# Mixer A's copy of q in the order of dilation 4: from ScalarE to GpSimd

## The chip, the core and the metric

The kernel runs on one core of a Trainium2 chip. The metric is the time of one execution in microseconds (us) on that core. The core has five engines that work side by side, each through its own instructions in the program's order: TensorE (PE; PEld is its weight load), VectorE (DVE), ScalarE (ACT), GpSimd (POOL) and SyncE (SP, which only issues DMAs here). They wait for each other by semaphores.

## The reference, cut to what matters

One layer of an encoder over 2048 tokens of width 1024: RMSNorm, one input projection, two mixers side by side (A: dilated window attention; B: latent attention), an output projection, a mixture of experts, a last RMSNorm. The change lies in mixer A. It has 8 heads of 64 columns, and each head attends three times, with windows of stride 1, 4 and 16:

```python
for window, dilation in ((128, 1), (512, 4), (2048, 16)):
    qr, kr, vr = to_residue(q), to_residue(k), to_residue(v)   # order by residue modulo the dilation
    scores = einsum('bhrnqd,bhrnkd->bhrnqk', qblk, kb) * dh ** -0.5
    scores = where(valid, scores + bias, NEG_INF)
    p = exp(scores - max(scores)); l = sum(p); o = p @ vb / l
# the three outputs are merged by their log-sum-exp weights
```

## The kernel before

The stages follow each other: `phase1` (input projection), `phase3` (mixer A), `mla` (mixer B), `phase5` (output projection), `moe` with `final`. In `phase3`, q of a head comes by DMA into the tile QA16, a [128, 2048] tile of fp16 in the order of dilation 16, which holds the two fp16 halves of q on 64 partitions each. The matmuls want q in 128 adjacent columns for each window, so `perm_q` copies it twice more on chip: into QA1 (order of dilation 1) and QA4 (order of dilation 4), in four pieces of 512 columns each. For QA4 a piece is written to 512 adjacent columns and read as 16 runs of 32 columns.

The work of a head is cut into 20 units: units 0 to 3 of dilation 16 (four windows each), 4 to 11 of dilation 1 and 12 to 19 of dilation 4 (two windows each); 8 heads make 160 units. One loop runs over steps s, and each step issues six parts of a pipeline, in this order:

- for the unit s: its `perm_q` piece, if it has one (QA1 in units 0 to 3, QA4 in units 4 to 7), then `qk` (PE, lines 681 and 682, into the PSUM tile S), `soft1` (DVE, line 706: adds the bias table and takes the row's extreme, into the tiles sb and st)
- for s-1: `soft2` (POOL, lines 723 and 729: subtracts the extreme, sb into pp)
- for s-2: `soft3` (ACT, line 733: exp, in place in pp)
- for s-3: `trans` (PE, line 746: transposes pp into PT; then ACT, line 757: the upper fp16 half, phi)
- for s-4: `low` (DVE, line 763: the lower half, plo)
- for s-5: `pv` (PE, lines 783 to 785, into O; at the end of a group of units ACT, line 788, copies O out into st)

The scheduler is switched off (`tc.manual_schedule()`): each engine runs its instructions in the order in which the program issues them. S has 3 buffers, sb 3, pp 4, and QA4 has one. QA16 alternates between two places from head to head.

POOL has two more duties in the stage. `scale_tables` (line 614) multiplies the bias tables by the scale of a pair of heads: in unit 12 of heads 1, 3 and 5 for the next pair (three instructions in a row), and twice within head 0 (steps 1 and 9). `put` (line 637) scales st three times for each pair, in steps that belong to units 8 and 16 of an odd head and unit 4 of the head after it, before SP stores st.

QA4 of a head is first read by `qk` of unit 12.

Of the kernel before, what the change touches and what calls it, by code (L numbers as in the profile page):

```python
# [17 lines left out]
AF = mybir.ActivationFunctionType  # L18
# [18 lines left out]
class K:  # L37
# [528 lines left out]
    def phase3(self):  # L566
        nc, tc, io, dr = self.nc, self.tc, self.io, self.dram
        with ExitStack() as ctx:
# [10 lines left out]
            def perm_q(h, pat, r):  # L579

                if r == 0:
                    Qs[h, pat] = q1.tile([128, S], F16, name=f"QA{pat}", bufs=1)
                Q, src = Qs[h, pat], Qs[h, 16]
                if pat == 1:
                    nc.scalar.activation(Q.rearrange("p (t c y) -> p t c y", c=16, y=8)[:, 4 * r:4 * r + 4],
                                         src.rearrange("p (c t y) -> p t c y", c=16, y=8)[:, 4 * r:4 * r + 4], AF.Copy)
                else:
                    nc.scalar.activation(
                        Q.rearrange("p (r t a y) -> p r t a y", r=4, t=4, a=4)[:, r],
                        src.rearrange("p (a r t y) -> p r t a y", a=4, r=4, t=4)[:, r], AF.Copy)  # L590

            def load_v(p):
                t = vs[p] = self.v0() if p % 2 == 0 else vp.tile([128, 63, 2, VW], F16, name="v")
# [199 lines left out]
            for s in range(NS + 5):  # L793
                if s < NS:
                    h, u = divmod(s, U)
                    if u < 4:
                        perm_q(h, 1, u)
                    elif u < 8:
                        perm_q(h, 4, u - 4)
                    if u == 1 and h + 1 < HA:  # L800
                        self.load_qk(h + 1, q1 if h % 2 == 0 else self.pre)
                    if u == 1 and h == HA - 1:
                        self.pre4(0)
                    if u in (10, 11) and h == HA - 1:
                        self.pre4(u - 9)
                    if u in (9, 16) and h == HA - 1:
                        self.pre_b(u // 16)
                    if u == 5 and h % 2 == 0 and h // 2 + 1 < 4:
                        load_v(h // 2 + 1)
                    if u == 12 and h % 2 and h // 2 + 1 < 4:  # L810
                        scale_tables(h // 2 + 1, (t16, t1, t4))
                    if s in (1, 9):
                        scale_tables(0, (t1,) if s == 1 else (t4,))
                    qk(s)
                    soft1(s)
# [1596 lines left out]
```

## Time and profile before

| | |
|---|---|
| median of 3 runs | 2306.95 us (2306.91 to 2308.32) |
| the profiled execution | 2312.83 us, of which the span of the profile is 2310.6 us |
| busy in the span | PE 2060.5, DVE 1666.5, ACT 1439.9, POOL 1092.7 us |
| mixer A's loop | first `perm_q` piece at 438.88 us, last part of the loop at 695.43 us |

Times are counted from the start of the span. In a row of the timeline stand the start, the busy time, the engine, the line, the operation, the tiles written and read, the shapes and how many were merged (x4); in brackets, the idle time of the engine just before and what ended it. Consecutive instructions of an engine overlap a little, so the distance from one start to the next is shorter than the busy time of one; the text calls that distance the pitch. A wait that several engines ended is put down to the one that came last by the profile. The row of a source line gives the shortest, median and longest duration in ns.

### The profile page before, as it was taken

Reading aid. Unit: us, or ns where it says so; the run is one execution under the profiler, and the core shown is the slowest. Engines: PE = TensorE matmul, PEld = TensorE weight load, DVE = VectorE, ACT = ScalarE, POOL = GpSimd, SP = SyncE. Lnnn points to the kernel's source line nnn. Section 1 sums busy time; section 2 is a strip of 40 time slices with the busy share of each in tenths; the row PEclk is TensorE's granted clock in tenths of the full one; section 3 lists DMA queues with packets and bytes.
Section 4 is the critical chain, followed back from the end, with each engine's and each line's share of the span. In section 5 each row is a group of like instructions: output and inputs, shape, how many; then the busy total and the mean of one; then the engine's idle time right before and its main releaser. Section 6 shows DMA issues by size and latency. Waiting matters only on the chain. (4 is left out here: it accounts for less than half of the span.)

```text
span 2310.6 us, 42905 instructions
## 1 busy us (share of the span) xinstructions
PE 2060.5 (89%) x16099; PEld 1458.3 (63%) x16099; DVE 1666.5 (72%) x3741; ACT 1439.9 (62%) x2125; POOL 1092.7 (47%) x1193
## 2 busy tenths in 40 slices
PE   5889989788889899999999999898888899999990
PEld 3458434577778466665655655577776588788870
DVE  7732221488887788888888899968787577777765
ACT  5532211499997588888888878744343366667653
POOL 1110000377763255555555556644654656667740
PEclk9989989999999899999999999899998999999995
DMA  4412344956735100000000221154444789999978
GB/s 153 131 54 68 123 151 122 224 139 153 163 100 154 37 20 22 6 22 21 7 22 9 55 93 24 34 165 143 150 147 147 219 298 293 291 308 319 311 211 308
DMA packets 196676, 312.81 MB, mean 135 GB/s; under 512 B 64185, under 2 KB 149090, under 8 KB 183460
## 3 DMA queue, kind: packets, MB, share of 16 engines
q1 hardware_dynamic: 166420, 174.43, 26.4%
q0 software_dynamic: 29760, 134.85, 18.2%
q8 instruction: 127, 2.08, 0.4%
q14 instruction: 81, 0.66, 0.1%
q10 hardware_dynamic: 288, 0.79, 0.1%
HBM read 235.66 MB, written 101.25 MB: 146 GB/s over the span
## 5 line engine op out<-in xcount | busy, mean ns | idle before, releaser
L961 POOL TENSOR_TENSOR lo<-p,hi 128x512 f16<-128x512 f32 x256 | 343.0, 1344 | 295.5 <-ACT p L955 233.7
L954 ACT ACTIVATE hi<-S,mla_scale 128x1024 f16<-128x1024 f32 x256 | 285.5, 1115 | 135.0 <-PE S L949 133.4
L923 DVE TENSOR_REDUCE part<-M 128x1 f32<-128x512 f32 x512 | 340.4, 680 | 13.1 <-PE M L921 11.7
L955 ACT ACTIVATE p<-S,mla_scale 128x1024 f32<-128x1024 f32 x256 | 285.2, 1114 | 0.0
L960 DVE TENSOR_TENSOR lo<-p,hi 128x512 f16<-128x512 f32 x256 | 228.9, 895 | 12.1 <-ACT p L955 10.3
L983 PE MATMUL O<-VB,lo 128*128 128x65 f16 x2048 | 198.9, 194 | 6.8 <-DVE lo L960 4.3
L978 PEld LDWEIGHTS <-hi 128*128 128x128 f16 x2048 | 184.9, 98 | 27.0 <-issue 21.5
L978 PE MATMUL O<-VB,hi 128*128 128x129 f16 (+1 forms) x2048 | 198.9, 215 | 0.0
L983 PEld LDWEIGHTS <-lo 128*128 128x128 f16 x2048 | 177.7, 99 | 17.4 <-DVE lo L960 5.9
L729 POOL TENSOR_TENSOR pp<-sb,st 128x256 f32<-128x256 f32 (+1 forms) x256 | 142.9, 581 | 45.1 <-DVE st L706 32.9
L2117 DVE TENSOR_TENSOR s<-raw,s 128x1024 fp32r<-128x1024 f32 x120 | 140.2, 1221 | 17.1 <-ACT s L2115 16.0
L1425 PE MATMUL pm<-s,mT_hi 128*128 128x512 f32 x512 | 137.3, 415 | 3.8 <-ACT mT_hi L1410 3.8
L2074 PE MATMUL pd<-s,hT 128*128 128x512 f32 x540 | 138.2, 404 | 1.7 <-ACT hT L2061 1.7
L614 POOL TENSOR_SCALAR t<-t,a_scale 128x512 f32<-128x512 f32 (+1 forms) x12 | 16.1, 1354 | 261.3 <-DMA t<-d_r 245.2
L2161 POOL DMA_INDIRECT d_x<-o,rec x47 | 88.1, 1874 | 106.7 <-ACT s L2115 33.7
L365 DVE SCALAR_TENSOR_TENSOR qk_sb<-pm,wscale,qk_sb 128x512 f16<-128x512 f32 x32 | 24.0, 750 | 149.3 <-ACT qk_sb L364 149.3
L746 PE MATMUL PT<-ident,pp 128*128 128x128 f32 (+1 forms) x640 | 104.5, 287 | 25.6 <-ACT pp L733 24.0
L2115 ACT ACTIVATE s<-raw 128x1024 fp32r<-128x1024 f32 x120 | 118.2, 1049 | 12.8 <-DMA raw<-in_w_up,eidx 6.8
L733 ACT ACTIVATE pp<-pp,a_scale 128x512 f32<-128x512 f32 (+1 forms) x160 | 114.0, 713 | 11.2 <-POOL pp L729 9.5
L2074 PEld LDWEIGHTS pd<-s,hT 128*128 128x128 f32 x540 | 101.2, 188 | 30.1 <-issue 4.3
L364 ACT ACTIVATE qk_sb<-pm,wscale 128x512 f16<-128x512 f32 x32 | 22.0, 688 | 153.4 <-DMA d_qk<-qk_sb 76.8
L1425 PEld LDWEIGHTS pm<-s,mT_hi 128*128 128x128 f32 x512 | 98.8, 198 | 26.1 <-ACT mT_hi L1410 4.1
(511 smaller groups left out, 5963.7 us busy)
## 6 DMA issues: line engine op xcount, KB each, us to landing
x<-in_x SPq DMA_DIRECT2D x32, 512.0 KB
na<-d_na SPq DMA_DIRECT2D x48, 264.0 KB
d_qk<-qk_sb SPq DMA_DIRECT2D x64, 128.0 KB
d_x<-x SPq DMA_DIRECT2D x16, 512.0 KB
d_h<-h SPq DMA_DIRECT2D x16, 512.0 KB
y<-d_x SPq DMA_DIRECT2D x16, 512.0 KB
out<-y SPq DMA_DIRECT2D x16, 512.0 KB
d_q<-qs SPq DMA_DIRECT2D x16, 384.0 KB
```

Source lines behind the costliest of these rows:

```text
L729: nc.gpsimd.tensor_sub(dst, src, res[:, s0 + i, 65:66, None, None].to_broadcast([128, 2, na, nx // 2]))
L923: nc.vector.tensor_reduce(part[m][:, qt, kc:kc + 1], ps, axis=AX.X, op=ALU.max)
L954: nc.scalar.activation(hi, ps, AF.Exp, scale=es)
L955: nc.scalar.activation(p32, ps, AF.Exp, scale=es)
L960: nc.vector.tensor_sub(lo[:, :, 0:LV], p32[:, :, 0:LV], hi[:, :, 0:LV])
L961: nc.gpsimd.tensor_sub(lo[:, :, LV:512], p32[:, :, LV:512], hi[:, :, LV:512])
L978: nc.tensor.matmul(o[:, c0:c0 + own], hi[:, j, q], V[:, 0:own], start=(kt == 0 and qt == 0), stop=False, skip_group_check=True)
L983: nc.tensor.matmul(o[:, c0:c0 + 65], lo[:, j, q], V[:, 0:65], start=False, stop=(kt == 15 and qt == 3), skip_group_check=True)
L1425: nc.tensor.matmul(ps[half], mT[a][:, j], wo[b][j // 2][:, j % 2, 512 * half:512 * half + 512], start=(n == 0), stop=(n == 23))
L2074: self.nc.tensor.matmul(ps[:, half], hT[a][:, j], w[b][:, j, 512 * half:512 * half + 512], start=(n == 0), stop=(n == len(k) - 1))
L2115: nc.scalar.activation(hi, src, AF.Copy)
L2117: eng.tensor_sub(lo, src, hi)
```

## The change

Only the copy into QA4 is touched: the same four pieces for each head, 32 in all, in the same place of the program's order, now as a copy on GpSimd. The copy into QA1 stays with ScalarE.

```diff
                 else:
-                    nc.scalar.activation(
+                    nc.gpsimd.tensor_copy(
                         Q.rearrange("p (r t a y) -> p r t a y", r=4, t=4, a=4)[:, r],
-                        src.rearrange("p (a r t y) -> p r t a y", a=4, r=4, t=4)[:, r], AF.Copy)
+                        src.rearrange("p (a r t y) -> p r t a y", a=4, r=4, t=4)[:, r])
```

## Rows read from the trace of the kernel before

**Rows 1.** Windows, mixer A: stretch, length, busy PE, PEld, DVE, ACT, POOL, clock, DMA

```profile
470.00:500.00 30.00, 24.92 (x360) 21.60 (x358) 23.18 (x94) 25.32 (x51) 23.65 (x39) 0.94 0.27 73
500.00:530.00 30.00, 27.82 (x431) 24.47 (x428) 27.70 (x120) 29.79 (x61) 23.13 (x39) 1.00 1.04 232
```

**Rows 2.** Waits from 440 to 690 us: total us, times, longest

```profile
PE PT L746 <- ACT pp L733: 24.0, 49, 2.9
...
ACT pp L733 <- POOL pp L729: 9.5, 4, 3.1
```

**Rows 3.** ScalarE's timeline, head 2: first and last copies, two exps, next head

```profile
500.61 0.62 ACT L585 ACTIVATE QA<-QA 128x512 f16<-128x512 f16 x1
...
507.31 0.64 ACT L588 ACTIVATE QA<-QA 128x512 f16<-128x512 f16 x1
507.83 0.73 ACT L733 ACTIVATE pp<-pp,a_scale 128x512 f32<-128x512 f32 x1
...
509.19 0.64 ACT L588 ACTIVATE QA<-QA 128x512 f16<-128x512 f16 x1
...
512.84 0.66 ACT L588 ACTIVATE QA<-QA 128x512 f16<-128x512 f16 x1
...
514.72 0.77 ACT L733 ACTIVATE pp<-pp,a_scale 128x512 f32<-128x512 f32 x1
...
519.73 0.79 ACT L733 ACTIVATE pp<-pp,a_scale 128x512 f32<-128x512 f32 x1
...
529.85 0.62 ACT L585 ACTIVATE QA<-QA 128x512 f16<-128x512 f16 x1
```

**Rows 4.** GpSimd's timeline in the same head, units 2 to 5 and 10

```profile
504.68 1.05 POOL L723 TENSOR_TENSOR pp<-sb,st 128x512 f32<-128x512 f32 x1 [0.39 <-DVE st L706]
506.12 1.05 POOL L723 TENSOR_TENSOR pp<-sb,st 128x512 f32<-128x512 f32 x1 [0.40 <-DVE st L706]
507.15 0.33 POOL L637 TENSOR_SCALAR st<-st,a_scale 128x32 f32<-128x32 f32 x1
507.43 0.97 POOL L729 TENSOR_TENSOR pp<-sb,st 128x192 f32<-128x192 f32 x2
509.20 1.18 POOL L729 TENSOR_TENSOR pp<-sb,st 128x256 f32<-128x256 f32 x2 [0.79 <-DVE st L706]
...
517.73 1.18 POOL L729 TENSOR_TENSOR pp<-sb,st 128x256 f32<-128x256 f32 x2 [0.19 <-DVE st L706]
```

**Rows 5.** TensorE's and VectorE's timelines in the same head

```profile
510.50 0.66 PE L746 MATMUL PT<-ident,pp 128*128 128x128 f32 x4 [0.42 <-ACT pp L733]
...
512.11 0.42 DVE L706 CUSTOM_DVE_ANT_0 sb<-S,t 128x256 f32<-128x256 f32 x1 [0.46 <-POOL pp L729]
...
515.77 0.42 DVE L706 CUSTOM_DVE_ANT_0 sb<-S,t 128x256 f32<-128x256 f32 x1 [0.46 <-POOL pp L729]
```

**Rows 6.** The copy on ScalarE, by its source line

```profile
L588 ACT ACTIVATE QA<-QA x32: 622/652/668, 444.6 to 668.7; 128x512 f16<-128x512 f16 x32
```

**Rows 7.** GpSimd's groups by shape, whole span: xcount, busy us, mean ns, idle before

```profile
L729 POOL TENSOR_TENSOR pp<-sb,st 128x256 f32<-128x256 f32 x176 | 104.3, 615 | 41.5 <-DVE st L706 30.3 <-ACT st L788 5.6 <-ACT pp L733 4.6
...
L723 POOL TENSOR_TENSOR pp<-sb,st 128x512 f32<-128x512 f32 x32 | 33.5, 1050 | 36.1 <-DVE st L706 31.7 <-PE S L682 4.4
...
L614 POOL TENSOR_SCALAR t<-t,a_scale 128x512 f32<-128x512 f32 x8 | 12.5, 1567 | 16.1 <-DMA t<-d_t 16.1
...
L1129 POOL COPY Kl<-s 32x512 f16<-32x512 f16 x4 | 2.4, 608 | 1.2 <-DVE s L1127 1.2
```

**Rows 8.** GpSimd's and ScalarE's timelines, head 1, the scaling of the tables

```profile
484.96 4.01 POOL L614 TENSOR_SCALAR t<-t,a_scale 128x256 f32<-128x256 f32 x3
...
490.16 0.72 ACT L733 ACTIVATE pp<-pp,a_scale 128x512 f32<-128x512 f32 x1 [3.09 <-POOL pp L729]
```

**Rows 9.** The same two timelines, head 0

```profile
441.09 4.07 POOL L723 TENSOR_TENSOR pp<-sb,st 128x512 f32<-128x512 f32 x4 [23.48 <-DVE st L706]
...
450.85 1.56 POOL L614 TENSOR_SCALAR t<-t,a_scale 128x512 f32<-128x512 f32 x1
...
454.18 0.75 ACT L733 ACTIVATE pp<-pp,a_scale 128x512 f32<-128x512 f32 x1
```

**Rows 10.** SyncE's timeline: the load of head 4's q into head 2's QA16

```profile
524.20 3.63 SPq L560 DMA_DIRECT2D QA<-d_qk  x2
```

## The prediction

> **What bounds the kernel now.** I began with the windows over mixer A [rows 1]. From 500 to 530 us ScalarE is busy 29.79 of 30 us, while GpSimd is busy 23.13 and VectorE and TensorE some 27.7; from 470 to 500 all of them drop, and GpSimd drops least. So the stage has two kinds of stretch: most of each head, where ScalarE is full, and a second one that has to be looked for. The waits [rows 2] agree: TensorE waits for the exp of line 733 (24.0 us in 49 waits), and ScalarE is seldom kept waiting by GpSimd (9.5 us in only 4 waits, so these few are long).
>
> Then head 2 in the timeline. On ScalarE [rows 3] a step of units 4 to 7 lasts 1.88 us (507.31 to 509.19), and of this the copy is 0.52 us (507.31 to 507.83), less than its own 652 ns [rows 6] because neighbours overlap. The head starts at 500.61 and the next at 529.85, that is 29.24 us. GpSimd in the same steps [rows 4] has 0.39 to 0.79 us of idle time ahead of each unit. It also runs ahead of ScalarE: it starts the subtraction of unit 2 at 504.68 and ends it 1.05 us later, at 505.73, while ScalarE's exp of unit 2 starts at 507.83. VectorE waits up to 0.46 us a unit [rows 5]; the rows name GpSimd, but TensorE's transposes of 510.50 wait for ScalarE, the scores of the next unit follow them in TensorE's order, and VectorE's part at 512.11 needs these. So in units 4 to 8 the whole ring goes at ScalarE's pace. From 517 us on VectorE has no gap, so there a lead that was won earlier is kept, not enlarged.
>
> The second kind is the scaling of the tables [rows 8]: 4.01 us on GpSimd in the middle of heads 1, 3 and 5, for which ScalarE idles 3.09 us. There the time of GpSimd's arrival counts.
>
> **What is removed.** 32 copies leave ScalarE. At a pitch of 0.52 us that is 2.08 us a head and 16.6 us in all, the most that the change can give. In units 4 to 8 the exps then start earlier by up to 2.08 us: that of unit 6 at 512.64 instead of 514.72, that of unit 10 at 517.65 instead of 519.73.
>
> **What is added.** 32 copies of 128x512 fp16 on GpSimd. The trace before has the same operation on 32 partitions, 512 columns of fp16 into fp16, at 608 ns [rows 7]. Below it I go no lower than 0.52 us, ScalarE's price. Above it are the two-input subtraction of 512 fp32 columns (1050 ns) and the one-input scaling of 512 fp32 columns (1567 ns). I take 0.60 us, the row with the same operation, type and number of columns; what differs is the number of partitions and that the copy reads 16 runs of 32 columns. The subtraction of line 729 reads in short runs as well and line 723 does not: 256 columns cost 615 ns and 512 cost 1050, which leaves no room for a price of the runs.
>
> The Trainium skill (GPSIMD Engine Reference, section 3.1) gives GpSimd about 2.6 cycles of 1.2 GHz for each element of an elementwise operation. By that figure a copy of 512 columns would be 1.11 us, an estimate from the page, and by the sum below the change would lose about 4 us. The row of 608 ns disagrees for a copy with one input.
>
> **The wait this adds.** Each copy is queued ahead of the subtraction of the unit before (soft2), behind which stand the exps of ScalarE and then TensorE's transposes. So I add up GpSimd's order of an even head from the end of unit 2's subtraction at 505.73 [rows 4]: four copies 4c, unit 3 1.05, the scaling of line 637 0.30 (0.33 busy, 0.28 to the next start), unit 4 0.97, units 5 to 10 six times 1.18, together 9.40 + 4c. GpSimd so ends unit 10 at 515.13 + 4c at the earliest. Before, it ended it at 517.73 + 1.18 = 518.91.
>
> - Even heads 2, 4, 6 and head 7. Unit 6 is ready at 505.73 + 1.05 + 0.30 + 0.97 + 2.36 + 4c, which with c = 0.60 is 512.81, and its signal about 0.05 later, against 512.64 on ScalarE: ScalarE waits 0.22. Unit 10 is ready at 517.53, before ScalarE wants it. Gain 2.08 - 0.22 = 1.86 each. With a larger c the gain is 519.73 - 0.05 - (515.13 + 4c) = 4.55 - 4c. Head 7 has no scaling of tables and ScalarE has extra work there, so I count it with these. Four heads: 7.4 us.
> - Odd heads 1, 3, 5. GpSimd starts on the tables right behind unit 10 [rows 8], so what counts is its own arrival: 518.91 - 517.53 = 1.38 in head 2's clock, 3.78 - 4c in general (line 637 falls into unit 8 there, the same sum). Three heads: 4.1 us.
> - Head 0. GpSimd starts late and is full [rows 9]: 4.07 us for units 0 to 3 from 441.09, then copies 2.40, units 4 to 7 4.51, the scaling of a table 1.56 and unit 8 1.18, which ends at 454.81. ScalarE's exp of unit 8 began at 454.18, so it comes 0.6 later. Some is made up in the rest of the head; I take a loss of 0.5, or 1.9 - 4c as a gain.
>
> The sum: 7.4 + 4.1 - 0.5 = 11.0 us, at c = 0.60. For c above 0.68 it is 4(4.55 - 4c) + 3(3.78 - 4c) + 1.9 - 4c = 31.4 - 32c: a tenth of a microsecond on the copy costs 3.2 us, and at 0.98 us nothing is left.
>
> Two edits I cost at nothing. QA4 is read from unit 12 on, some 8 us behind the last copy; the piece would have to be that late to matter. SP loads head 4's q over head 2's at 524.20 [rows 10]; GpSimd's last read of it ends near 511.7, so the load, which now waits for GpSimd instead of ScalarE, starts no later. If it did, it would have most of a head to land.
>
> What follows mixer A (projections, output, experts) hangs on it in order, and nothing in it waits for a fixed moment, so I carry the 11 us to the end: 2312.83 - 11 = 2301.8 for the profiled execution. The median of the runs lies 5.9 us below that execution, hence 2306.95 - 11 = 2296 us.
>
> **The rivals.**
>
> *The copy costs what a two-input operation costs* (1.05 us, line 723). For it: it is the nearest row with all 128 partitions and 512 columns. Against: two inputs, four bytes. The sum gives 31.4 - 33.6 = -2.2: 2309 us, no change to be told. 12 in 100. The figure of the Trainium skill's page above, 1.11 us, would be this case, with 4 us lost.
>
> *The copy costs what the scaling of the tables costs* (1.567 us), the case on the other side. Its place is units 4 to 10 of every head: GpSimd then becomes the engine that all others wait for. From 1.13 us on the kernel is slower by more than 0.2%; at 1.567 the sum is 31.4 - 50.1 = -18.7: 2326 us. For it: one input, as the copy has, and still slower than the subtraction. Against: it multiplies by a scalar in fp32, and the row with COPY is at 608. 7 in 100.
>
> *The next engine is the bound.* VectorE and TensorE are busy 27.7 of 30 us, so a head of 29.24 us can't go below about 27; with a lower c or a longer ring of waits the lead would shrink from unit 12 on. If half of the 11 us is lost so, 2301.5 us. For it: VectorE has no gap from 517 on. Against: its gaps lie in units 5 to 9, where the gain is made. 15 in 100.
>
> *The copies were hidden anyway* and nothing moves: 2307 us. Against: ScalarE's rows in units 4 to 8 have no idle time, and TensorE waits for them. 4 in 100.
>
> **How the numbers follow.** The forecast, a gain between about 7 and 14 us, has 62 in 100. What a measurement of this kernel can tell from no change is about 0.2%, 4.6 us. The third rival straddles that bound: 12 of its 15 go to faster, 3 to no change; the first and the fourth (16) go to no change, with 1 of the first to slower; the second (7) to slower. Faster 0.74, same 0.18, slower 0.08. The range: its low end is ScalarE's whole 16.6 us, 2290.5, which only a copy at 0.52 with no loss in head 0 would come near; its high end, 2305, takes in the third rival and a copy of up to 0.92 us.
>
> **What the profile after would show.** The copy as a POOL row near 0.6 us x32. ScalarE's steps of units 4 to 7 at about 1.36 us instead of 1.88, with its exp of unit 6 waiting a little for GpSimd. GpSimd without gaps from unit 4 to unit 9. Head 2 in 27.4 us instead of 29.24; head 0 not shorter; the waits of TensorE for line 733 fewer, those of ScalarE for line 729 more. The prediction falls if the copy is above 0.8 us, or if the lead of unit 10 is lost again before the next head starts, which would show as VectorE or TensorE waiting for each other in units 12 to 19.

## The result, and the profile after

The changed kernel takes 2293.86 us (median of 22 runs, 2287.43 to 2305.72), the kernel before 2306.64 (22 runs beside them, 2300.94 to 2314.23). The ratio is 0.9948, with a 95% interval of 0.9936 to 0.9960: 12.0 us faster, 9.2 to 14.8 (the ratio is of the means; the medians lie 12.8 apart). The forecast was 11 us and 2296.

The copy by its source line in the profile after:

```profile
L588 POOL COPY QA<-QA x32: 603/609/613, 440.2 to 650.4; 128x512 f16<-128x512 f16 x32
```

It is the price of the COPY row in [rows 7], on all 128 partitions and with the read in runs of 32 columns. ScalarE's timeline in head 2, against [rows 3] (all times 5.73 us earlier, since the head starts so much earlier):

```profile
494.88 0.62 ACT L585 ACTIVATE QA<-QA 128x512 f16<-128x512 f16 x1
...
501.59 0.73 ACT L733 ACTIVATE pp<-pp,a_scale 128x512 f32<-128x512 f32 x1
...
502.94 0.74 ACT L733 ACTIVATE pp<-pp,a_scale 128x512 f32<-128x512 f32 x1
...
506.91 0.77 ACT L733 ACTIVATE pp<-pp,a_scale 128x512 f32<-128x512 f32 x1
...
511.91 0.79 ACT L733 ACTIVATE pp<-pp,a_scale 128x512 f32<-128x512 f32 x1
...
522.04 0.62 ACT L585 ACTIVATE QA<-QA 128x512 f16<-128x512 f16 x1
```

The steps of units 4 to 7 now take 1.35 us (501.59 to 502.94, the exps of units 2 and 3) where they took 1.88. The exps of units 6 and 10 (506.91 and 511.91) come 12.03 and 17.03 us after the head's start, where they came 14.11 and 19.12 after it. That is 2.08 and 2.09 us gained, ScalarE's whole share, and the head is 27.16 us instead of 29.24: nothing of it is lost by the head's end.

GpSimd's timeline in the same head, against [rows 4]:

```profile
498.95 1.05 POOL L723 TENSOR_TENSOR pp<-sb,st 128x512 f32<-128x512 f32 x1 [0.40 <-DVE st L706]
499.94 0.61 POOL L588 COPY QA<-QA 128x512 f16<-128x512 f16 x1
500.51 1.05 POOL L723 TENSOR_TENSOR pp<-sb,st 128x512 f32<-128x512 f32 x1
...
504.99 0.61 POOL L588 COPY QA<-QA 128x512 f16<-128x512 f16 x1
505.56 7.92 POOL L729 TENSOR_TENSOR pp<-sb,st 128x256 f32<-128x256 f32 x14
513.78 2.19 POOL L729 TENSOR_TENSOR pp<-sb,st 128x256 f32<-128x256 f32 x4 [0.31 <-DVE st L706]
```

From the first copy at 499.94 to 513.48 GpSimd has no gap; before, it waited ahead of most units. A copy takes 0.57 us from start to start (499.94 to 500.51), and two subtractions back to back take 1.13 (7.92 us for 14), not the 1.18 of two that stand alone. So unit 10 is done at 505.56 + 5 x 1.13 = 511.2, in time for the exp at 511.91.

The odd heads: GpSimd's scaling of the tables and ScalarE's exp behind it in head 1, against [rows 8]:

```profile
479.27 4.00 POOL L614 TENSOR_SCALAR t<-t,a_scale 128x256 f32<-128x256 f32 x3
```

```profile
484.45 0.72 ACT L733 ACTIVATE pp<-pp,a_scale 128x512 f32<-128x512 f32 x1 [3.29 <-POOL pp L729]
```

GpSimd comes to the tables 16.41 us after the head's start (462.86) instead of 18.27 (466.69 to 484.96), 1.86 us earlier. The stall itself stays: 3.29 us of ScalarE's time, 3.09 before.

From here on one measure serves for all runs, worked out from the timelines: a head lasts from its first QA1 piece to that of the next, the last one to the start of the last copy of O (line 788); the loop is their sum. Both kernels were profiled three times, the second and third time as the runs e7, e8, e11 and e12:

| us | head 0 | 1 | 2 | 3 | 4 | 5 | 6 | 7 | loop |
|---|---|---|---|---|---|---|---|---|---|
| before | 27.81 | 33.92 | 29.24 | 34.73 | 29.24 | 33.56 | 29.09 | 38.96 | 256.55 |
| before (e7) | 27.61 | 32.38 | 29.23 | 32.02 | 29.23 | 32.02 | 29.09 | 39.07 | 250.65 |
| before (e11) | 27.79 | 32.39 | 29.22 | 33.52 | 29.23 | 33.54 | 29.09 | 38.96 | 253.74 |
| after | 27.90 | 32.02 | 27.16 | 32.76 | 27.17 | 31.64 | 27.01 | 35.95 | 241.61 |
| after (e8) | 27.93 | 32.05 | 27.17 | 32.81 | 27.17 | 31.66 | 27.04 | 35.96 | 241.79 |
| after (e12) | 27.91 | 31.78 | 27.16 | 30.16 | 27.16 | 31.32 | 27.02 | 37.06 | 239.57 |

On average the loop is 253.65 us before and 240.99 after: 12.7 us, and the timed runs say 12.0. The time from the loop to the end of the span is not the same in any two traces (1610.7 to 1615.2 us before, 1615.6 to 1621.4 after); three traces of each don't tell whether the few us between are chance. In the traces of the experiments below it is 1618.7 us with the copy on ScalarE (e9), 1612.1 with no copy at all (e1) and 1610.3 with two on GpSimd (e3), so it does not go by the copy's engine alone; what sets it is open.

### The profile page after: what moved, and what is told of

Same layout as the page of the kernel before. It is cut to its first block, busy times and chain, and to the rows that moved or that the text cites. A ratio compares the mean times of both kernels' runs of the same rounds, so it can differ in the third digit from the quotient of the medians.

```text
span 2298.0 us, 42911 instructions
## 1 busy us (share of the span) xinstructions
PE 2051.4 (89%) x16099; PEld 1457.0 (63%) x16099; DVE 1656.8 (72%) x3741; ACT 1422.5 (62%) x2093; POOL 1113.4 (48%) x1225
## 3 DMA queue, kind: packets, MB, share of 16 engines
q8 instruction: 127, 2.08, 0.4%
## 5 line engine op out<-in xcount | busy, mean ns | idle before, releaser
L923 DVE TENSOR_REDUCE part<-M 128x1 f32<-128x512 f32 x512 | 340.5, 680 | 13.6 <-PE M L921 12.4
```

The source lines that it names most:

```text
L923: nc.vector.tensor_reduce(part[m][:, qt, kc:kc + 1], ps, axis=AX.X, op=ALU.max)
```

## The experiments

**GpSimd's part alone, and ScalarE's part alone.** e2 keeps the copy on ScalarE and adds the same one on GpSimd, into a scratch tile:

```diff
                         src.rearrange("p (a r t y) -> p r t a y", a=4, r=4, t=4)[:, r], AF.Copy)
+                    jk = wk.tile([128, 512], F16, name="qjunk", bufs=1)
+                    nc.gpsimd.tensor_copy(
+                        jk.rearrange("p (t a y) -> p t a y", t=4, a=4),
+                        src.rearrange("p (a r t y) -> p r t a y", a=4, r=4, t=4)[:, r])
```

> The kernel before, copy on ScalarE kept, with GpSimd making the same copies as well into a scratch tile that nobody reads. So it adds GpSimd's part alone. Theory: GpSimd runs 2 to 3 us ahead of ScalarE and has 0.4 to 0.8 us idle a unit, so even heads stay at 29.24 us, odd ones within 0.3 us of before; head 0 up to 2 us longer; 0 to 3 us slower than before. Rival (each copy on GpSimd delays the subtraction behind it and so the ring): 4 x 0.57 = 2.3 us a head, 18 us slower.

Measured: ratio to before 0.9999 (0.9983 to 1.0016); heads 2, 4 and 6 29.24, 29.24 and 29.10 us, head 0 27.92. The 32 copies cost nothing that the interval, some 4 us to either side, can tell. The timeline of GpSimd in head 2 of this run, whose lines are four further down:

```profile
506.97 1.05 POOL L727 TENSOR_TENSOR pp<-sb,st 128x512 f32<-128x512 f32 x1 [0.39 <-DVE st L710]
507.96 0.61 POOL L592 COPY qjunk<-QA 128x512 f16<-128x512 f16 x1
...
513.57 1.19 POOL L733 TENSOR_TENSOR pp<-sb,st 128x256 f32<-128x256 f32 x2
514.98 1.18 POOL L733 TENSOR_TENSOR pp<-sb,st 128x256 f32<-128x256 f32 x2 [0.22 <-DVE st L710]
```

The gaps of [rows 4] are filled, and by unit 7 (514.98) GpSimd waits for VectorE again: it has caught up.

e1 leaves the copy out altogether; dilation 4 then reads QA16 as it is, so only its time is of use:

```diff
+                if pat == 4:
+                    Qs[h, 4] = Qs[h, 16]
+                    return
```

> Leaves the copy into QA4 out on every engine: dilation 4 reads QA16 as it is, so the order of q is wrong there and the output with it. It takes 32 copies from ScalarE and adds nothing to GpSimd. Theory (ScalarE's pitch in units 4 to 8 was the bound, and GpSimd takes the copies out of its lead): the even heads stay at the 27.1 us of the changed kernel, the odd ones are at most 0.3 us shorter than there, head 0 is 1 to 2 us shorter; all in all 1 to 3 us under the changed kernel, 0.55 to 0.65% under the kernel before. Rival (GpSimd's copies still hold the ring up, and the 12 us are what is left of a larger gain): even heads under 26.8 us, and 4 us or more under the changed kernel.

Measured: 0.9929 (0.9907 to 0.9951). Heads 2, 4 and 6 are 27.15, 27.17 and 27.02 us, those of the changed kernel; head 0 is 26.03 (27.9 there), the odd ones 31.83, 31.43 and 31.14. So in an even head GpSimd's copies cost nothing against no copies at all, and they use up 1.9 us in head 0, where GpSimd starts late and is full. The rival's 26.8 us did not come. By the ratios e1 lies 4.4 us under the changed kernel, more than the 1 to 3 us expected and as much as the rival asked; its own interval is 5 us to either side, and in the loops (238.86 us against 240.99) it is 2.1 us, nearly all of it head 0.

**Doubling the price.** e3 makes each GpSimd copy twice, the second time into the scratch tile:

```diff
                         src.rearrange("p (a r t y) -> p r t a y", a=4, r=4, t=4)[:, r])
+                    jk = wk.tile([128, 512], F16, name="qjunk", bufs=1)
+                    nc.gpsimd.tensor_copy(
+                        jk.rearrange("p (t a y) -> p t a y", t=4, a=4),
+                        src.rearrange("p (a r t y) -> p r t a y", a=4, r=4, t=4)[:, r])
```

> The changed kernel with each GpSimd copy made twice, the second time into a scratch tile: doubles the price c to 1.14 us. Theory: GpSimd's lead is used up; by its order unit 6 is ready some 2.0 us after ScalarE wants it, so even heads are at 28.7 to 29.3 us, odd heads 0 to 0.5 us longer than before, head 0 about 2 us longer; 0 to 5 us slower than before, 12 to 17 us slower than the changed kernel. Rival (GpSimd at 48% of the span has room for it): as the changed kernel, 12 us under before.

Measured: 1.0040 (1.0024 to 1.0056), 9.2 us slower than before, above what was expected. Heads 2, 4 and 6 are 29.19, 29.21 and 29.06 us, head 0 30.13: the lead is spent and the whole gain is gone, as the order of GpSimd said. ScalarE now waits for GpSimd in units 5 and 6 of head 2:

```profile
513.23 0.72 ACT L737 ACTIVATE pp<-pp,a_scale 128x512 f32<-128x512 f32 x1 [0.87 <-POOL pp L733]
...
515.48 0.72 ACT L737 ACTIVATE pp<-pp,a_scale 128x512 f32<-128x512 f32 x1 [0.77 <-POOL pp L733]
```

But the loop of this trace, 256.64 us, is no longer than the first one before, so the kernel was profiled once more (e10).

> The kernel with two GpSimd copies for each piece once more. Its timed runs were 9 us above the kernel before although the loop of its profile was as long as the one before. Theory: the clock falls behind the stalls of all odd heads in most executions, which the first trace missed in head 1: odd heads 34 to 35 us, the loop 257 to 260 us. Rival: the loop is 256 us again and the time is lost elsewhere.

Measured: loop 260.55 us, odd heads 35.32, 35.09 and 33.74. The mean of the two loops is 258.6, 4.9 us above the mean before: 2.4 in head 0, the rest in the odd heads. The interval of the timed runs begins at 5.5 us, so part of the 9.2 lies outside the loop or in the scatter of the stalls. The first trace was of the fastest of e3's nine runs (2307.63 us, median 2315.35), that of e10 took 2318.56; more than that these runs don't say.

**The scatter of the stalls.** e7 and e11 are the kernel before, e8 and e12 the changed one, unaltered.

> The kernel before once more, for the scatter of the heads between executions. Theory: heads 2, 4, 6 at 29.24 us within 0.05; the odd heads and head 7, where the clock falls after a stall, between 32 and 35 and between 36 and 39.5 us.

> The changed kernel once more, for the same. Theory: heads 2, 4, 6 at 27.1 us within 0.1; the odd heads between 30 and 33 us, head 7 between 34 and 37.5.

> The kernel before a third time, for how often the clock falls behind its stalls. Theory: heads 2, 4, 6 at 29.24 us; the odd heads at either of two lengths, 32 to 32.4 us where the clock stays at its upper level and 33.5 to 34.8 where it falls.

> The changed kernel a third time, for the same. Theory: heads 2, 4, 6 at 27.1 us; the odd heads at 31.6 to 32.8 us where the clock falls and some 1.5 us less where it does not.

Measured as in the table. The even heads repeat within 0.03 us. An odd head has three lengths, by whether the clock falls behind the stall and for how long: of the changed kernel's, 30.16 us where it did not fall, 31.3 to 32.1 where it fell, 32.8 where it stayed down twice as long (head 3 of the first trace and of e8). Windows over the stall in head 3, the same distance from the head's start, first in the first trace after (32.76 us), then in e12 (30.16 us); the eighth value is the granted clock:

```profile
540.00:544.00 4.00, 1.36 (x23) 1.12 (x20) 2.11 (x9) 0.72 (x2) 4.00 (x5) 0.92 0.13 29
544.00:548.00 4.00, 3.59 (x30) 3.25 (x31) 1.79 (x8) 3.12 (x7) 2.85 (x7) 0.50 0.00 0
548.00:552.00 4.00, 4.00 (x55) 3.87 (x53) 2.69 (x11) 2.95 (x7) 2.53 (x6) 0.73 0.02 6
```

```profile
541.62:545.62 4.00, 1.35 (x22) 1.11 (x20) 2.12 (x9) 0.72 (x2) 4.00 (x5) 1.00 0.12 28
545.62:549.62 4.00, 3.61 (x59) 3.42 (x60) 2.95 (x13) 4.00 (x9) 4.00 (x9) 1.00 0.00 0
```

The stall is the same in both: TensorE was busy 1.36 and 1.35 us of 4. In the first the clock then fell to 0.50, its lower level of 1.2 GHz, in the second it stayed at 2.4, and the head was 2.6 us shorter. Of nine odd heads the clock fell behind the stall in five before and in eight after. Where it fell for as long in both, the change gained 1.9 to 2.0 us (33.92 to 32.02 in head 1, 34.73 to 32.76 in head 3); where it did in neither, 1.9 too (32.02 to 30.16 in head 3).

**Taking the stall away.** e5 is the changed kernel with the tables scaled in small parts; e9 is the same edit in the kernel before:

```diff
-                    if u == 12 and h % 2 and h // 2 + 1 < 4:
-                        scale_tables(h // 2 + 1, (t16, t1, t4))
+                    if h // 2 + 1 < 4 and u in (1, 13, 17):
+                        t = {1: t16, 13: t1, 17: t4}[u]
+                        c = 2 * (h // 2 + 1) + h % 2
+                        nc.gpsimd.tensor_scalar(t[:, c:c + 1], t[:, c:c + 1], self.asc[:, h // 2 + 1, 0:1], None, op0=ALU.mult)
```

> The changed kernel with the tables of the next pair scaled one head's part at a time, in units 1, 13 and 17 of heads 0 to 5, instead of three whole tables in unit 12 of heads 1, 3 and 5. Theory (what keeps the odd heads 4 to 5 us longer is GpSimd's block and the lower clock that follows the stall): odd heads fall from 32 to between 27.2 and 28.2 us, no granted clock under 0.95 after unit 12, even heads at most 0.8 us longer; 8 to 14 us under the changed kernel. Rival (with the copies GpSimd is full, and the scaling costs its 5.6 us a pair wherever it stands): under 4 us gained, the even heads longer by what the odd ones lose.

> The kernel before (copy on ScalarE) with the tables scaled as in the spread version, a part in units 1, 13 and 17 of heads 0 to 5. It parts the gain of the copy from that of the tables. Theory: the odd heads fall to about 29.3 us like the even ones; 9 to 13 us under the kernel before; against the spread version with the copy on GpSimd 12 to 16 us slower, so that the change is worth about 2.08 us in nearly every head where no stall stands in between. Rival (the change only made room for the scaling): the odd heads stay above 31 us and less than 5 us are gained.

Measured: e5 0.9897 (0.9879 to 0.9915), 2284.07 us, the fastest of all; e9 0.9958 (0.9944 to 0.9972). The odd heads are 27.45 us in e5 and 29.5 in e9; the even ones 27.0 to 27.25 and 29.1 to 29.3. The loop is 229.60 against 243.20. So with no stall in between, the copy's move is worth 13.6 us: 2.05 to 2.07 in each of heads 1 to 6, 1.82 in head 7, -0.60 in head 0. By the ratios it is 14 us. In e5 the clock stays up where head 1 stalled:

```profile
484.00:488.00 4.00, 4.00 (x72) 3.80 (x71) 4.00 (x18) 3.94 (x9) 4.00 (x8) 1.00 0.02 4
488.00:492.00 4.00, 3.70 (x63) 3.48 (x60) 3.67 (x16) 3.53 (x7) 4.00 (x9) 1.00 0.57 165
```

**Other engines.** e4 puts the copy into QA1 on GpSimd as well:

```diff
-                    nc.scalar.activation(Q.rearrange("p (t c y) -> p t c y", c=16, y=8)[:, 4 * r:4 * r + 4],
-                                         src.rearrange("p (c t y) -> p t c y", c=16, y=8)[:, 4 * r:4 * r + 4], AF.Copy)
+                    nc.gpsimd.tensor_copy(Q.rearrange("p (t c y) -> p t c y", c=16, y=8)[:, 4 * r:4 * r + 4],
+                                         src.rearrange("p (c t y) -> p t c y", c=16, y=8)[:, 4 * r:4 * r + 4])
```

> The changed kernel with the copy into QA1 on GpSimd as well (64 copies there, none on ScalarE). Theory: what holds a head of 27.1 us is no longer ScalarE alone: VectorE and TensorE are full from unit 9 on, and GpSimd's order grows by 2.3 us a head; even heads 26.5 to 27.2 us, odd heads between 1 us shorter and 1 us longer; within 4 us of the changed kernel. Rival (ScalarE is the bound of the whole head): 2.08 us a head again, 16 us under the changed kernel.

Measured: 0.9945 (0.9925 to 0.9964), as the changed kernel; heads 2, 4 and 6 27.31, 27.32 and 27.17 us, 0.15 longer than there. Another 2.08 us a head off ScalarE gain nothing, but the edit does two things at once: GpSimd has no gap from 498.23 to 518.04 in head 2, and ScalarE now waits for it, as in units 4 and 5:

```profile
508.04 0.62 ACT L733 ACTIVATE pp<-pp,a_scale 128x384 f32<-128x384 f32 x1 [0.29 <-POOL pp L729]
...
509.74 0.72 ACT L733 ACTIVATE pp<-pp,a_scale 128x512 f32<-128x512 f32 x1 [0.32 <-POOL pp L729]
```

So GpSimd has no room for eight copies a head. Whether relieving ScalarE further would still gain something with the copies elsewhere is not shown: no run takes the QA1 copies away without giving them to GpSimd.

e6 has the change's copy on VectorE:

```diff
-                    nc.gpsimd.tensor_copy(
+                    nc.vector.tensor_copy(
```

> The changed kernel with the 32 copies on VectorE instead of GpSimd. Theory: VectorE has about 0.3 us idle a unit in units 4 to 8 at ScalarE's old pace and none at the new one, so a copy of 0.2 to 0.65 us makes it the bound there: even heads 27.6 to 29.2 us, 0 to 12 us slower than the changed kernel, depending on the price of the copy. Rival (any engine but ScalarE will do): the same 27.16 us a head.

Measured: 0.9963 (0.9950 to 0.9976), 8.5 us faster than before; heads 2 and 4 28.16 and 28.14. The copy there:

```profile
L588 DVE COPY QA<-QA x32: 448/608/911, 439.0 to 655.5; 128x512 f16<-128x512 f16 x32
```

On the median it costs as much as on GpSimd, on an engine with less room: VectorE is busy 8.00 of 8 us from 500 to 508 us, and half of the gain of a head is left. What the rows say of why it takes so long there is told at the end.

## Why the prediction was right, point by point

- *ScalarE is the bound in units 4 to 8.* Shown: taking its copies away alone (e1) and replacing them (the change) give the same even heads, and adding the GpSimd copies alone (e2) gives nothing and costs nothing.
- *The copy costs 0.60 us.* 609 ns, 0.57 from start to start. By the prediction's estimate from the Trainium skill (GPSIMD Engine Reference, section 3.1), about 2.6 cycles for each element, it would have been 1.11. That section says further on that its figure is that of tensor_tensor, with two inputs; applying it to a copy was the mistake, and 609 ns says nothing against the figure itself. The same page's section 4.1 calls operations with one input roughly line-rate, to which 512 columns in 609 ns come nearer.
- *GpSimd's order uses up the lead; at 0.98 us the gain is gone.* Borne out on both sides by two prices: at 0.57 all of it is there, at 1.14 (e3) the even heads are back at 29.2 us; the crossing itself was not tried. That e3's even heads fit the sum so well is in part luck. For dearer copies the sum takes the lead at unit 10, 4.55 - 4c, but unit 6 binds ahead of it: by the prediction's own terms the gain there is 4.26 - 4c, as its 1.86 at 0.60 shows. In e3 ScalarE does wait at units 5 and 6 and no later, and the order up to unit 6 is shorter than summed, 4.46 us beside the copies instead of 4.68. The two errors nearly cancel. The sum's 5.1 us of loss at 1.14 stand beside 4.9 in the loops and 9.2 in the timed runs (interval from 5.5).
- *Even heads 1.86 us.* Measured 2.07. The term that was mis-sized is GpSimd's order: 11.80 us from unit 2 to unit 10, by pitches of operations that stood alone; back to back it took 511.2 - 500.0 = 11.2, and ScalarE's wait of 0.22 did not come.
- *Odd heads 1.38 us.* The mean of three traces each is 99.4 us for the three heads before and 95.4 after, 1.32 a head. The agreement is partly luck: like for like it is 1.9, as GpSimd came to the tables 1.86 us earlier and not 1.38, for the same reason as in the even heads; and the clock fell more often after than before. (The prediction reads from [rows 1] that GpSimd drops least from 470 to 500 us; in those rows it rises, from 23.13 to 23.65, which fits the tables no less.)
- *Head 0 loses 0.5 us.* It lost 0.2 on average. The 1.7 us that ScalarE gains there without any copy (e1) are used up by GpSimd, as the prediction had it; but the exp of unit 8 comes 15.58 us after the head's start instead of 15.30, 0.28 late and not 0.6.
- *Head 7 as the even heads.* It gained 2.7 us on average of three (36.0, 36.0 and 37.1 against 39.0). Where the clock falls in it, and for how long, differs from trace to trace: in e12, where it is as in the traces before, the gain is 1.9 to 2.0. The 1.82 of the pair e5 and e9 is not like for like either, as the clock stayed down longer in e5.
- *Nothing of it is lost behind mixer A.* Loop 12.7, timed 12.0; by the mean spans of the three traces each, 2304.0 and 2294.7, only 9.3. No loss beyond the scatter can be told.
- *The rival that the next engine is the bound* is wrong for this step. For the next one e4 shows only that GpSimd is full. VectorE is busy in all of the last 14.73 us of the changed kernel's head 2 (507.31 to 522.04), ScalarE in 14.52 and TensorE in 14.64; which of them would bind then was not tried.

## What to carry to other kernels

To move work to another engine, add up that engine's own order between two points where it is known to be ready, and compare it with when the next engine asks: here GpSimd was 2 to 3 us ahead, and 2.3 us of copies fitted in, 4.5 (e3) did not. Take the price from a row with the same operation, type and number of inputs, and the pitch from instructions that stand back to back. And when the bound of the usual part of a loop has been lowered, look at its unusual parts: spreading three scalings of tables gained 9.7 us (e9), nearly as much as the change.

## What had not been expected of the hardware

The copy on VectorE took 448 to 911 ns where the same one on GpSimd took 603 to 613. VectorE's timeline in head 2 of e6, and GpSimd's:

```profile
500.25 0.85 DVE L588 COPY QA<-QA 128x512 f16<-128x512 f16 x1
...
502.18 0.47 DVE L588 COPY QA<-QA 128x512 f16<-128x512 f16 x1
...
503.86 0.61 DVE L588 COPY QA<-QA 128x512 f16<-128x512 f16 x1
```

```profile
499.90 1.05 POOL L723 TENSOR_TENSOR pp<-sb,st 128x512 f32<-128x512 f32 x1 [0.40 <-DVE st L706]
...
501.52 0.98 POOL L729 TENSOR_TENSOR pp<-sb,st 128x192 f32<-128x192 f32 x2 [0.22 <-DVE st L706]
503.13 1.18 POOL L729 TENSOR_TENSOR pp<-sb,st 128x256 f32<-128x256 f32 x2 [0.63 <-DVE st L706]
```

GpSimd's subtractions end at 500.95, 502.50 and 504.31; the three copies end at 501.10, 502.65 and 504.47. So it is in all 28 copies of heads 1 to 7: each starts while GpSimd subtracts and ends 0.14 to 0.16 us after that subtraction does, whether the copy took 464 ns or 851. It looks as if the copy needs some 0.15 us and spends the rest waiting for GpSimd, though the records name no wait. The Trainium skill (SBUF — State Buffer, Who interferes with whom) says that a copy on VectorE in a two-port mode and an instruction of GpSimd block each other, and the later one waits for the whole of the other; these rows agree, though they don't show in which mode the copy ran. A copy on VectorE while GpSimd is idle was not tried.

That the clock can stay up behind a stall as long as one behind which it falls, as in head 3 of e12 and of the first trace, was not foreseen either. Why it falls more often in the changed kernel (eight of nine against five) is open. In e1, e4 and e6, whose even heads are shorter than before's as well, it fell in all nine odd heads, in e2, e3 and e10, whose even heads are at the old pace, in seven of nine. That is too little for a proof.
